# Sixteen products without use in front of the second unit's key norm, in both halves of a hybrid decoder block

## The chip, the cores and the metric

The kernel runs on one core of one Trainium2 chip. The metric is the device time of one execution in microseconds; of several executions the median counts. The engines are named as in the profile: PE (TensorE), PEld (its weight loads), DVE (VectorE), ACT (ScalarE), POOL (GpSimd) and SP (SyncE, which issues most transfers).

## What is computed

One decoder layer on a sequence of 1024 tokens with 1024 channels, all in fp32. The conditioning vector c gives shift, scale and gate of two sub-layers. The first is a token mixer of two parallel branches:

```python
h = rms_norm(x, norm1_gain) * (1 + scale1) + shift1
proj = h @ w_in
cols = proj[..., :q_lo]; cols = cols + (token_shift(cols) - cols) * tshift_mu
y_a = rwkv7_time_mix(cols, ...)        # 8 heads of 64, delta-rule state
y_b = sliding_window_sink_attention(...)   # 8 query heads, window 128
merged = gate_a * (y_a @ w_branch_a) + gate_b * (y_b @ w_branch_b)
x = x + gate1 * (merged @ w_out)
```

The second is a SwiGLU feed-forward block. In the RWKV branch each head's key direction is divided by its length; this is the key norm:

```python
kk = heads(k * k_k)
kk = kk / jnp.maximum(jnp.sqrt(jnp.sum(kk * kk, axis=-1, keepdims=True)), 1e-12)
```

## The kernel before, in words

**Halves and units.** The mixer goes through two halves of 512 tokens (the loop over h), and in each through four units (p = 0 to 3), a unit being two RWKV heads on 128 partitions. The branch projections to 1024 channels, the output projection and the feed-forward block follow.

**Products.** An fp32 product is made of three: both operands are split into a high and a low part, and `mm3` (L138 to L144) issues low weight by high activation, high by low, and high by high, each a matmul of 128x512. `proj_block` (L473) makes one block of 128 columns of `w_in` from eight such triples, 24 products, in a PSUM tile `pg` of a pool of two. Each unit starts with three such blocks: key, receptance, value, in this order. `shifted` (L483) then mixes each with its neighbour token: a copy on ACT (`tm`, L489), two small copies on POOL, and one operation on DVE (`rvk`, L491).

**The unit.** `rwkv_unit` (L494) starts with two low-rank products, `pz` (L499) and `paa` (L505). ACT takes `pz` through a tanh into `sz` (L501) and `paa` into `ath` (L507). POOL and DVE make the cumulated decay `cum` of `sz` (L511), and ACT its exponentials, `wpad` (L515) and `winv` (L517). Then ACT squares the scaled keys (`sq`, L522), and PE sums the squares of each head: `ns` (L524), a product of fp32 operands, which the trace shows as two passes. ACT copies its two rows to `nrow` (L526), and they go through memory to the later stages. Further products of the unit are `bs` (L561, from `ath` on DVE), `pa` and `pk`. `pz`, `paa`, `ns`, `bs`, `pa` and `pk` share a PSUM pool `pm` of two buffers, so each waits until the tile two before it has been read.

**Work beside it.** `ada_rest` (L872 to L886) makes the rest of the conditioning, eight times a call, one call for each unit: SP loads a tile `adaw` (L883, one buffer), ACT scales it (L884), POOL adds it (L885). ACT goes through its instructions in order, so all that stands behind L884 waits for that load. Attention is dealt in between the units (`mixer_step`); the keys of an attention block are rounded by ACT to `kdup` (L802), DVE makes the low part `klo` (L803), and PE makes the scores `sc` (L827).

**What sets the order.** The code is written unit by unit; a tile scheduler, which has a model and priorities of its own, deals the instructions to each engine's order when the kernel is built. An instruction that is added or tied to another changes what is dealt behind it.

Of the kernel before, what the change touches and what calls it, by code (L numbers as in the profile page):

```python
# [10 lines left out]
F32 = mybir.dt.float32  # L11
# [8 lines left out]
P = 128  # L20
D = 1024
S = 1024
HALF = 512
NH = 2
KT = D // P
RW = 512
NP = 4
NPOOL = 3
NC = HALF // 64
DFF = 2816  # L30
NJ = DFF // P
# [35 lines left out]
def block_kernel(ctx: ExitStack, tc: tile.TileContext, a: dict, out: bass.AP):  # L67
    nc = tc.nc
# [15 lines left out]
    def vcol(name, i=0, n=1):  # L84
        st, r0, cnt = ROWS[name]
        return vT[st][:, r0 + i:r0 + i + n]
# [53 lines left out]
    def mm3(ps, lh, ll, rh, rl, first, last, more=False):  # L140

        nc.tensor.matmul(ps, lhsT=ll, rhs=rh, start=first, stop=False, skip_group_check=more)  # L142
        nc.tensor.matmul(ps, lhsT=lh, rhs=rl, start=False, stop=False, skip_group_check=more)  # L143
        nc.tensor.matmul(ps, lhsT=lh, rhs=rh, start=False, stop=last, skip_group_check=more)  # L144

    gates_d = dr.tile([NH, 16, P, HALF], F32, name="gates_d")
    ya_d = dr.tile([NH, NP, P, HALF], F32, name="ya_d")
    yb_d = dr.tile([NH, NP, P, HALF], F32, name="yb_d")
    a_scr = dr.tile([NH, NP, 2, NC, 2, 32, 32], F32, name="a_scr")
    t_scr = dr.tile([NH, NP, 2, NC, 2, 32, 32], F32, name="t_scr")  # L150
    n_scr = dr.tile([NH, NP, 2, HALF], F32, name="n_scr")
# [25 lines left out]
    with ExitStack() as mx:  # L177
# [5 lines left out]
        pm = mx.enter_context(tc.tile_pool(name="pm", bufs=2, space=PSUM))  # L183
# [84 lines left out]
        with tc.tile_pool(name="su", bufs=1, side="right") as su:  # L268
# [24 lines left out]
            def ada_columns(g, wts):  # L293

                pcol = pc.tile([P, 4], F32, tag="pc", name="pcol")
                for sec in range(2):
                    acc = su.tile([P, 256], F32, tag="adacc", name="adacc", bufs=3)
                    if sec == 0 and g < NPOOL:
                        nc.gpsimd.memset(acc, 0.0)
# [5 lines left out]
                    else:  # L305
                        nc.vector.tensor_scalar(out=acc, in0=wts[sec][:, 0, :],
                                                scalar1=vcol("c", 0), scalar2=None, op0=ALU.mult)
                    for k in range(1, 0 if sec == 0 and g < NPOOL else KT):
                        nc.vector.scalar_tensor_tensor(out=acc, in0=wts[sec][:, k, :],
# [40 lines left out]
            blk1 = wc.tile([P, P], F32, name="blk1")  # L350
# [122 lines left out]
        def proj_block(hT, j):  # L473

            wh, wl = w_block(j)
            del w_ahead[j]
            pool, tag = first_psum.pop(j, (pg, "pg"))
            ps = pool.tile([P, HALF], F32, tag=tag, name="pg")
            for k in range(KT):
                mm3(ps, wh[:, k, :], wl[:, k, :], hT[k][0], hT[k][1], k == 0, k == KT - 1)  # L480
            return ps

        def shifted(hT, j, dst):  # L483

# [6 lines left out]
                nc.vector.scalar_tensor_tensor(out=dst, in0=ps, scalar=ommu[:, j:j + 1],  # L491
                                               in1=tm[:, 0:HALF], op0=ALU.mult, op1=ALU.add)

        def rwkv_unit(h, p, rvk, xwa, sgx):  # L494
            r_, v_, k_ = (rvk[:, i, :] for i in range(3))

            ch = slice(p * P, (p + 1) * P)
# [22 lines left out]

            sq = wk.tile([P, HALF], F32, tag="early", name="sq", bufs=5)
            nc.scalar.activation(out=sq, in_=k_, func=AF.Square, scale=vcol("k_k", p))  # L522
            ns = pm.tile([2, HALF], F32, tag="pm", name="ns")
            nc.tensor.matmul(ns, lhsT=blk1[:, 0:P:64], rhs=sq, start=True, stop=True)  # L524
            nrow = wk.tile([2, HALF], F32, tag="early", name="nrow", bufs=5)
            nc.scalar.copy(out=nrow, in_=ns)  # L526
            nc.sync.dma_start(out=n_scr[h, p], in_=nrow)
# [40 lines left out]
            for b in range(2):  # L568
                pas = [pm.tile([P, 4, P], F32, tag="pm", name="pa") for _ in range(2)]
                for c4 in range(4):  # L570
                    c = 4 * b + c4
                    for q in range(2):
                        rows = slice(64 * q, 64 * q + 64)
                        nc.tensor.matmul(pas[q][:, c4, :], lhsT=kb[rows, c, q:q + 2, :],
                                         rhs=ar[rows, c, :, :], start=True, stop=True)
# [30 lines left out]
            for sl in range(2):  # L606
# [5 lines left out]
                for jj in range(16):  # L612
# [3 lines left out]
                    m, n = j // 4 + 1, 31 - j  # L616
# [24 lines left out]
            for c in range(NC):  # L641
                for q in range(2):
                    u0 = 64 * (1 - q)
                    nc.tensor.matmul(pv1[u0 + 32:u0 + 64, c, :],
                                     lhsT=asb[q][u0:u0 + 32, c, 32:64], rhs=tn[u0:u0 + 32, c, :],
                                     start=True, stop=True)
# [3 lines left out]
            for c in range(NC):  # L650
                for q in range(2):
                    u0 = 64 * (1 - q)
                    nc.tensor.matmul(pt1[u0:u0 + 32, c, :], lhsT=v1[u0 + 32:u0 + 64, c, :],
                                     rhs=tt[u0 + 32:u0 + 64, c, 32:64], start=True, stop=True)
# [4 lines left out]
            for c in range(NC):  # L659
                g = G[p]  # L660
                zp = pc.tile([P, 64], F32, tag="pc", name="zp")
                for q in range(2):
# [3 lines left out]
                                     start=True, stop=False)  # L666
                for q in range(2):
# [3 lines left out]
                                     start=False, stop=True)  # L671
# [5 lines left out]
                up = pc.tile([P, 64], F32, tag="pc", name="up")  # L677
                for q in range(2):
# [3 lines left out]
                                     start=True, stop=True)  # L682
# [3 lines left out]
                for q in range(2):  # L686
                    rows = slice(64 * q, 64 * q + 64)
                    nc.tensor.matmul(gp[rows, :], lhsT=kbt[q][:, c, :], rhs=vu[q][:, c, :],
                                     start=True, stop=True)
# [4 lines left out]
                for q in range(2):  # L694
                    rows = slice(64 * q, 64 * q + 64)
                    nc.tensor.matmul(yps[rows, c, :], lhsT=ar[rows, c, 1, :], rhs=g[rows, :],
                                     start=True, stop=False)
                for q in range(2):
                    rows = slice(64 * q, 64 * q + 64)
                    nc.tensor.matmul(yps[rows, c, :], lhsT=asb[q][:, c, 64:128], rhs=vu[q][:, c, :],  # L700
                                     start=False, stop=True)
# [16 lines left out]
            for q in range(2):  # L718
                rows = slice(64 * q, 64 * q + 64)
                pt = py.tile([P, NC, 64], F32, tag="py", name="pyt")  # L720
                for c in range(NC):
# [4 lines left out]
                    elif lo_ < 0:  # L726
                        nc.tensor.matmul(pt[64:128, c, :], lhsT=ycf[rows, 0:64],
                                         rhs=ident[rows, rows], start=True, stop=True)
# [166 lines left out]
        for h in range(NH):  # L895
            if h == 0:
                hT = hT0
            else:
                hT = []
# [9 lines left out]
            xwa = wk.tile([P, HALF], F32, tag="xwa", name="xwa", bufs=1)  # L909
            shifted(hT, 12, xwa)  # L910
            nc.scalar.activation(out=xwa[0:64, :], in_=xwa[0:64, :], func=AF.Tanh)
            sgx = wk.tile([P, HALF], F32, tag="sgx", name="sgx", bufs=1)
# [4 lines left out]
            for p in range(NP):  # L917
                mixer_step(h, p, hT)
                rvk = wk.tile([P, 3, HALF], F32, tag="rvk", name="rvk", bufs=2)
                for i, j in ((2, 4 + p), (0, p), (1, 8 + p)):  # L920
                    shifted(hT, j, rvk[:, i, :])
                rwkv_unit(h, p, rvk, xwa, sgx)
                if h == 0:
                    if p == 0:
                        rotary_tables()
                    prepare_x(p)
                ada_rest(4 * h + p)
# [17 lines left out]
            for j in range(16):  # L945
                ps = proj_block(hT, 20 + j)
# [523 lines left out]
```

## Time and profile before

| | |
|---|---|
| median of three runs | 1655.84 us (1649.59 to 1656.13) |
| profiled execution | 1638.24 us |
| its span | 1636.5 us |
| mean granted clock of PE in it | 0.989 |
| PE busy | 1553.0 us (95%), 8835 matmuls |
| DVE busy | 1192.2 us (73%) |
| ACT busy | 709.1 us (43%) |
| POOL busy | 156.1 us (10%) |
| chain of work that ended last | PE 73%, DVE 11%, DMA 6%, ACT 4% |

Busy shares are means over the span. The granted clock of PE stands as a share of its full speed: 1.00 is 2.4 GHz, and 0.50 is 1.2 GHz. The page counts a matmul of 128x512 with the time from its start to the end of its flow; the spacing of two starts is shorter, since matmuls overlap.

### The profile page before, as it was taken

The page shows a single profiled execution, that of the slowest core. Times are in us where ns is not written, and L with a number is a line of the kernel's source. Part 1 is how long each engine was busy: PE and PEld are TensorE (multiplying, and loading weights), DVE is VectorE, ACT ScalarE, POOL GpSimd, SP SyncE. Part 2 cuts the span into 40 slices and gives each one's busy share as a digit, 9 for nine tenths or more (in the row PEclk, how much of TensorE's full clock was granted, in tenths as well). Part 3 has the DMA queues.
Part 4 walks back from the last instruction along what each step waited for, and adds up shares of the span by engine and source line. Part 5 has one row for each costly group of instructions (what it writes and reads, how often), then busy time and mean ns, then how long its engine had stood idle before and what let it go on. Part 6 is the DMA issues. An engine that isn't in the chain of part 4 may idle for free.

```text
span 1636.5 us, 24815 instructions
## 1 busy us (share of the span) xinstructions
PE 1553.0 (95%) x8835; PEld 1195.9 (73%) x8835; DVE 1192.2 (73%) x2844; ACT 709.1 (43%) x1346; POOL 156.1 (10%) x220
## 2 busy tenths in 40 slices
PE   3978999999998999999999998999999999999998
PEld 2756776666665678667778886788888888888887
DVE  6689777877557868877368877976666677897465
ACT  6454343555744333446411566423333333444442
POOL 6223121212343000000000000000000000000000
PEclk9999999999999999999999999999999999999999
DMA  9345444544544323324583146253333232974441
GB/s 320 101 120 146 123 139 121 155 128 145 152 139 112 85 69 95 99 86 146 167 282 119 59 157 223 87 171 104 103 97 104 97 102 94 313 242 131 149 142 52
DMA packets 225502, 223.97 MB, mean 137 GB/s; under 512 B 38466, under 2 KB 162508, under 8 KB 225380
## 3 DMA queue, kind: packets, MB, share of 16 engines
q1 hardware_dynamic: 225380, 222.41, 44.4%
q8 instruction: 69, 1.13, 0.3%
q14 instruction: 53, 0.43, 0.1%
HBM read 171.73 MB, written 50.63 MB: 136 GB/s over the span
## 4 chain that ended last, share of the span: by engine, by line
PE 73%; DVE 11%; DMA 6%; ACT 4%; issue 2%; POOL 2%; SPq 1%; ACTq 0%; DVEq 0%; POOLq 0%
PE pgf L142 10%; PE pgf L143 10%; PE pgf L144 10%; PE pgo L144 6%; PE pgo L143 6%; PE pgo L142 6%; DMA adaw<-in_ada_w_dram 4%; PE pg L142 4%; PE pg L143 4%; PE pg L144 4%; PE pgq L142 1%; PE pgq L144 1%; PE pgq L143 1%; DVE rt L623 1%; DVE tmpi L619 1%
## 5 line engine op out<-in xcount | busy, mean ns | idle before, releaser
L142 PE MATMUL pg<-hhi,wlo 128*128 128x512 f32 x480 | 201.0, 421 | 2.0 <-DVE xwa L491 0.9
L143 PE MATMUL pg<-hlo,whi 128*128 128x512 f32 x480 | 198.8, 414 | 0.0
L144 PE MATMUL pg<-hhi,whi 128*128 128x512 f32 x480 | 198.2, 413 | 0.0
L144 PE MATMUL pgo<-wpart 128*128 128x512 f32 x420 | 163.9, 390 | 0.0
L143 PE MATMUL pgo<-wpart 128*128 128x512 f32 x420 | 163.8, 390 | 0.0
L142 PE MATMUL pgo<-wpart 128*128 128x512 f32 x420 | 163.3, 390 | 0.0
L133 ACT CAST whi<-wraw 128x1024 fp32r<-128x1024 f32 (+1 forms) x88 | 85.0, 967 | 98.2 <-PE pgf L144 45.0
L134 DVE TENSOR_TENSOR wlo<-wraw,whi 128x1024 fp32r<-128x1024 f32 (+1 forms) x88 | 100.9, 1146 | 26.0 <-ACT whi L133 18.0
L885 POOL TENSOR_TENSOR aacc<-aacc,adaw 128x512 f32<-128x512 f32 x64 | 90.6, 1416 | 257.6 <-ACT adaw L884 246.8
L142 PEld LDWEIGHTS pg<-hhi,wlo 128*128 128x128 f32 x480 | 92.5, 193 | 28.4 <-issue 6.7
L1066 DVE TENSOR_TENSOR u<-pgf,u 128x512 f32<-128x512 f32 x88 | 60.5, 689 | 68.0 <-PE pgf L144 67.1
L144 PEld LDWEIGHTS pg<-hhi,whi 128*128 128x128 f32 x480 | 92.8, 193 | 22.2 <-issue 3.3
L143 PEld LDWEIGHTS pg<-hlo,whi 128*128 128x128 f32 x480 | 92.9, 193 | 19.2 <-issue 1.3
L1061 ACT CAST wpart<-s 128x512 fp32r<-128x512 f32 x88 | 54.7, 622 | 111.0 <-PE pgf L144 99.8
L1061 ACT CAST wpart<-fo 128x512 fp32r<-128x512 f32 x77 | 48.0, 624 | 113.9 <-PE pgo L144 107.9
L1062 DVE TENSOR_TENSOR wpart<-fo,wpart 128x512 fp32r<-128x512 f32 x77 | 52.8, 687 | 52.4 <-ACT wpart L1061 52.3
L143 PEld LDWEIGHTS pgo<-wpart 128*128 128x128 f32 x420 | 78.8, 188 | 16.3 <-issue 0.2
L144 PEld LDWEIGHTS pgo<-wpart 128*128 128x128 f32 x420 | 78.9, 188 | 16.2
L142 PEld LDWEIGHTS pgo<-wpart 128*128 128x128 f32 x420 | 78.8, 188 | 16.2
L1061 ACT CAST wpart<-wraw 128x512 fp32r<-128x512 f32 x66 | 40.6, 622 | 101.3 <-PE pgf L144 98.6
L619 DVE SCALAR_TENSOR_TENSOR tmpi<-ai,inv,rt 128x60 f32<-128x60 f32 (+24 forms) x248 | 74.3, 300 | 10.6 <-DMA ai<-a_scr 6.9
L884 ACT ACTIVATE adaw<-adaw,vT 128x512 f32<-128x512 f32 x64 | 46.2, 722 | 73.2 <-DMA adaw<-in_ada_w_dram 67.7
(507 smaller groups left out, 3807.3 us busy)
## 6 DMA issues: line engine op xcount, KB each, us to landing
wraw<-in_w_in_dram SPq DMA_DIRECT2D x72, 512.0 KB
wraw<-in_ffn_w_dram SPq DMA_DIRECT2D x56, 512.0 KB
f_d<-fs SPq DMA_DIRECT2D x77, 256.0 KB
fo<-f_d SPq DMA_DIRECT2D x77, 256.0 KB
adaw<-in_ada_w_dram SPq DMA_DIRECT2D x64, 256.0 KB
w2t<-in_ffn_w_dram SPq DMA_DIRECT2D x44, 256.0 KB
adaw<-in_ada_w_dram SPq DMA_DIRECT2D x8, 1024.0 KB
gates_d<-gt SPq DMA_DIRECT2D x32, 256.0 KB
```

The costliest lines, as they stand in the source:

```text
L133: nc.scalar.copy(out=hi, in_=raw)
L134: nc.vector.tensor_tensor(out=lo, in0=raw, in1=hi.bitcast(F32), op=ALU.subtract)
L142: nc.tensor.matmul(ps, lhsT=ll, rhs=rh, start=first, stop=False, skip_group_check=more)
L143: nc.tensor.matmul(ps, lhsT=lh, rhs=rl, start=False, stop=False, skip_group_check=more)
L144: nc.tensor.matmul(ps, lhsT=lh, rhs=rh, start=False, stop=last, skip_group_check=more)
L619: nc.vector.scalar_tensor_tensor(out=tv, in0=ai[:, jj, j + 1:32].unsqueeze(1).broadcast_to([P, m, n]), scalar=inv2[:, j:j + 1], in1=rt[:, ...
L623: nc.vector.tensor_tensor(out=rt[:, 0:m, j + 1:32], in0=rt[:, 0:m, j + 1:32], in1=tv, op=ALU.add)
L884: nc.scalar.activation(out=wt, in_=wt, func=AF.Copy, scale=vcol("c", k))
L885: nc.gpsimd.tensor_tensor(out=acc, in0=acc, in1=wt, op=ALU.add)
L1061: nc.scalar.copy(out=hi, in_=src)
L1062: nc.vector.tensor_tensor(out=lo, in0=src, in1=hi.bitcast(F32), op=ALU.subtract)
L1066: nc.vector.tensor_tensor(out=out, in0=x, in1=y, op=op)
```

## The change

With `WARM` = 16, `proj_block` keeps the last product of the latest block (`proj_end`; for a unit this is its value block). In unit 1 of each half `keep_warm` takes a tile `pwarm` of `pm` and issues 16 products of 128x512 into it, all with the same weights (the first 128 columns of the first high part of the activations) and each with the high part of another block as its moving operand. Nothing reads them. Each is tied behind the one before it, the first behind `proj_end`, and `ns` behind the last of them, by a dependency that sets only the order.

```diff
+WARM = 16
...
             for k in range(KT):
-                mm3(ps, wh[:, k, :], wl[:, k, :], hT[k][0], hT[k][1], k == 0, k == KT - 1)
+                end = mm3(ps, wh[:, k, :], wl[:, k, :], hT[k][0], hT[k][1], k == 0, k == KT - 1)
+            proj_end[0] = end
             return ps
+
+        proj_end = [None]
+
+        def keep_warm(hT, n):
+
+            ps = pm.tile([P, HALF], F32, tag="pm", name="pwarm")
+            behind = proj_end[0]
+            for i in range(n):
+                mm = nc.tensor.matmul(ps, lhsT=hT[0][0][:, 0:P], rhs=hT[i % KT][0], start=True,
+                                      stop=True)
+                tc.add_manual_dep(mm.ins, behind.ins.name,
+                                  mybir.DependencyInfo(mybir.DependencyClass.NoSync,
+                                                       mybir.DependencyReason.DATA),
+                                  reason="right behind the projections")
+                behind = mm
+            return behind
...
             nc.scalar.activation(out=sq, in_=k_, func=AF.Square, scale=vcol("k_k", p))
+            warm = keep_warm(hT, WARM) if p == 1 else None
             ns = pm.tile([2, HALF], F32, tag="pm", name="ns")
-            nc.tensor.matmul(ns, lhsT=blk1[:, 0:P:64], rhs=sq, start=True, stop=True)
+            mm = nc.tensor.matmul(ns, lhsT=blk1[:, 0:P:64], rhs=sq, start=True, stop=True)
+            if warm is not None:
+                tc.add_manual_dep(mm.ins, warm.ins.name,
+                                  mybir.DependencyInfo(mybir.DependencyClass.NoSync,
+                                                       mybir.DependencyReason.DATA),
+                                  reason="behind the products that keep the clock up")
```

PE gets 32 instructions more. Its order is the one of before up to the first of the new products and again for its last 3329 instructions; between them the mixer's instructions are dealt anew on every engine. In the changed file the lines stand 1 lower from L30 on, 18 lower around `pz` and 24 lower behind `ns`.

PE in the first half, from `pz` of the second unit to its `ns`, before (27 products `pg` in nine triples, of which the first two and the last stand here):

```order
L499 MATMUL pz<-xwa,diu 128x512
L505 MATMUL paa<-xwa,diu 128x512
L142 MATMUL pg<-hhi,wlo 128x512
L143 MATMUL pg<-hlo,whi 128x512
L144 MATMUL pg<-hhi,whi 128x512
L142 MATMUL pg<-hhi,wlo 128x512
L143 MATMUL pg<-hlo,whi 128x512
L144 MATMUL pg<-hhi,whi 128x512
...
L142 MATMUL pg<-hhi,wlo 128x512
L143 MATMUL pg<-hlo,whi 128x512
L144 MATMUL pg<-hhi,whi 128x512
L524 MATMUL ns<-sq,blk_463 2x512
```

and after:

```order
L145 MATMUL pg<-hhi,whi 128x512
L492 MATMUL pwarm<-hhi 128x512 x16
L143 MATMUL pg<-hhi,wlo 128x512
L144 MATMUL pg<-hlo,whi 128x512
L145 MATMUL pg<-hhi,whi 128x512
L143 MATMUL pg<-hhi,wlo 128x512
L144 MATMUL pg<-hlo,whi 128x512
L145 MATMUL pg<-hhi,whi 128x512
L143 MATMUL pg<-hhi,wlo 128x512
L144 MATMUL pg<-hlo,whi 128x512
L543 MATMUL ns<-sq,blk_463 2x512
```

Ahead of these rows `pz`, `paa` and one triple stand as before, of which the first row here is the last product. So 11 products `pg` stand between `paa` and `ns` where 27 stood, and 16 stand behind `ns` that stood in front of it.

PE in the second half, same place, after:

```order
L517 MATMUL pz<-xwa,diu 128x512
L523 MATMUL paa<-xwa,diu 128x512
L143 MATMUL pg<-hhi,wlo 128x512
L144 MATMUL pg<-hlo,whi 128x512
L145 MATMUL pg<-hhi,whi 128x512
L492 MATMUL pwarm<-hhi 128x512 x16
L543 MATMUL ns<-sq,blk_463 2x512
```

Before, 17 products `pg` stood between `paa` and `ns` there and no others; 14 of them have moved behind `ns`. In both halves the first `pwarm` waits for a signal of ACT, the end of `sz`, which reads `pz` out of the buffer that `pwarm` takes.

ACT around the keys of the first attention block, before:

```order
L792 CAST qs_3863<-pq 64x512
L949 ACTIVATE gt<-pg,hbg 128x512
L605 COPY rt<-idpat 128x256
L884 ACTIVATE adaw_3419<-adaw_3419,vT_67 128x512
L802 CAST kdup_529<-pkT 64x128 x2
L802 CAST kdup_530<-pkT 64x128 x2
```

and after:

```order
L816 CAST qs_3877<-pq 64x512
L816 CAST qs_3880<-pq 64x512
L826 CAST kdup_529<-pkT 64x128 x2
L134 CAST whi<-wraw 128x1024
L826 CAST kdup_530<-pkT 64x128 x2
L672 COPY v_2399<-pv_2398 32x256 x2
L908 ACTIVATE adaw_3436<-adaw_3436,vT_67 128x512
```

The scaled copy of a load of `adaw` that stood right in front of `kdup` is behind it now. Elsewhere on ACT the opposite happened: in front of the third unit's `tm` and `sz` of the first half, where one copy of `adaw` stood, there are two. The orders of ACT and SP up to `sq` of the second unit in the first half are the ones of before.

## Rows read from the trace of the kernel before

**Rows 1.** The page, its span and its first part.

```profile
span 1636.5 us, 24815 instructions
...
PE 1553.0 (95%) x8835; PEld 1195.9 (73%) x8835; DVE 1192.2 (73%) x2844; ACT 709.1 (43%) x1346; POOL 156.1 (10%) x220
```

**Rows 2.** Waits of PE: engine, line, waited for; us in total, times, longest.

```profile
PE ns L524 <- ACT sq L522: 16.2, 6, 6.1
...
PE sc L827 <- DVE klo L803: 4.3, 1, 4.3
```

**Rows 3.** PE timeline, first half: start us, us, what, [idle before, releaser].

```profile
112.98 0.40 PE L144 MATMUL pg<-hhi,whi 128*128 128x512 f32 x1
119.51 1.86 PE L524 MATMUL ns<-sq,blk 128*2 128x512 f32 x2 [6.13 <-ACT sq L522]
121.31 0.80 PE L142 MATMUL pg<-hhi,wlo 128*128 128x512 f32 x1
...
124.86 0.40 PE L144 MATMUL pg<-hhi,whi 128*128 128x512 f32 x1
```

**Rows 4.** PE timeline, second half, around the second unit's key norm.

```profile
503.72 0.40 PE L144 MATMUL pg<-hhi,whi 128*128 128x512 f32 x1
503.96 0.39 PE L142 MATMUL pg<-hhi,wlo 128*128 128x512 f32 x1
504.19 0.40 PE L143 MATMUL pg<-hlo,whi 128*128 128x512 f32 x1
509.56 1.86 PE L524 MATMUL ns<-sq,blk 128*2 128x512 f32 x2 [4.97 <-ACT sq L522]
511.35 0.80 PE L144 MATMUL pg<-hhi,whi 128*128 128x512 f32 x1
...
514.02 0.40 PE L144 MATMUL pg<-hhi,whi 128*128 128x512 f32 x1
```

**Rows 5.** PE timeline, third unit of the first half.

```profile
150.30 1.02 PE L524 MATMUL ns<-sq,blk 128*2 128x512 f32 x2 [1.84 <-ACT sq L522]
...
161.57 1.34 PE L561 MATMUL bs<-ath,blk 128*128 128x512 f32 x2 [3.04 <-DVE ath L558]
...
163.56 0.63 PE L144 MATMUL pg<-hhi,whi 128*128 128x512 f32 x1
163.99 0.63 PE L142 MATMUL pg<-hhi,wlo 128*128 128x512 f32 x1
```

**Rows 6.** ACT timeline, first half, second unit.

```profile
110.11 0.69 ACT L501 ACTIVATE sz<-pz,hw 128x512 f32<-128x512 f32 x1
...
117.61 0.72 ACT L884 ACTIVATE adaw<-adaw,vT 128x512 f32<-128x512 f32 x1 [4.17 <-DMA adaw<-in_ada_w_dram]
...
118.75 0.70 ACT L522 ACTIVATE sq<-rvk,vT 128x512 f32<-128x512 f32 x1
```

**Rows 7.** ACT timeline, second half, second unit.

```profile
500.93 0.69 ACT L501 ACTIVATE sz<-pz,hw 128x512 f32<-128x512 f32 x1
...
506.53 0.72 ACT L884 ACTIVATE adaw<-adaw,vT 128x512 f32<-128x512 f32 x1 [4.34 <-POOL wpad L514]
```

**Rows 8.** Windows: us, PE, PEld, DVE, ACT, POOL busy (instructions), clock, DMA share, GB/s.

```profile
119.50:124.70 5.20, 5.19 (x10) 2.81 (x11) 5.02 (x10) 2.76 (x4) 1.77 (x3) 0.50 0.17 51
...
150.30:158.30 8.00, 8.00 (x32) 5.65 (x32) 6.88 (x25) 3.32 (x7) 1.20 (x3) 1.00 0.55 150
162.40:165.70 3.30, 3.30 (x9) 2.32 (x8) 3.30 (x14) 0.00 (x0) 0.00 (x0) 0.50 0.18 66
...
509.60:513.80 4.20, 4.20 (x8) 2.01 (x9) 4.09 (x12) 1.20 (x2) 1.06 (x1) 0.50 0.21 63
...
113.00:165.00 52.00, 40.33 (x185) 27.39 (x184) 47.28 (x137) 24.59 (x40) 14.01 (x19) 0.91 0.50 132
560.00:760.00 200.00, 198.40 (x1783) 143.63 (x1783) 154.30 (x592) 82.94 (x195) 3.04 (x9) 1.00 0.30 87
```

**Rows 9.** ACT timeline in front of the first attention block's keys.

```profile
285.03 0.72 ACT L884 ACTIVATE adaw<-adaw,vT 128x512 f32<-128x512 f32 x1 [4.82 <-DMA adaw<-in_ada_w_dram]
```

**Rows 10.** PE timeline, that block's scores.

```profile
288.14 0.30 PE L827 MATMUL sc<-klo,qs 128*128 128x128 f32 x1 [4.29 <-DVE klo L803]
```

More of the change, by code (lines that the diff above doesn't have):

```diff
@@ L143, in mm3 @@
         nc.tensor.matmul(ps, lhsT=lh, rhs=rl, start=False, stop=False, skip_group_check=more)
-        nc.tensor.matmul(ps, lhsT=lh, rhs=rh, start=False, stop=last, skip_group_check=more)
+        return nc.tensor.matmul(ps, lhsT=lh, rhs=rh, start=False, stop=last, skip_group_check=more)
     gates_d = dr.tile([NH, 16, P, HALF], F32, name="gates_d")
@@ L492, in shifted, with rwkv_unit @@
                                                in1=tm[:, 0:HALF], op0=ALU.mult, op1=ALU.add)
-        def rwkv_unit(h, p, rvk, xwa, sgx):
+        def rwkv_unit(h, p, rvk, xwa, sgx, hT):
             r_, v_, k_ = (rvk[:, i, :] for i in range(3))
@@ L921, in block_kernel @@
                     shifted(hT, j, rvk[:, i, :])
-                rwkv_unit(h, p, rvk, xwa, sgx)
+                rwkv_unit(h, p, rvk, xwa, sgx, hT)
                 if h == 0:
```

## The prediction

> **What bounds the kernel now.** I read the page first. PE is busy for 95% of the span and no other engine for more than 73% [rows 1], so almost all that PE does, it does on the path. The waits of PE came second. They show where PE stands still: the largest sum is its wait for `sq` in front of the key norm `ns`, 16.2 us in six times, the longest 6.1 [rows 2]. The timelines place two of the six in the second units: 6.13 us in the first half and 4.97 in the second [rows 3, 4]. Together that is 11.1 us of idle time in front of the two places that the change touches.
>
> Third came the clock. Behind the two waits the granted clock is 0.50, the lower level (1.2 GHz), for some 5.2 and 4.2 us [rows 8], where it was at full speed before the wait; `ns` then takes 1.86 us, while the third unit's `ns`, which came after an idle time of 1.84 us at a clock of 1.00, takes 1.02 [rows 5, 8]. Behind an idle time of 3.04 us in front of `bs` the clock is 0.50 too [rows 5, 8].
>
> Last, what PE waits for. `sq` is in order behind a scaled copy of `adaw` on ACT, which in the first half waited 4.17 us for its load and starts at 117.61; `sq` follows at 118.75 and ends at 119.45, when `ns` begins [rows 3, 6]. In the second half the copy waited 4.34 us for POOL [rows 7]. Neither wait is for PE. So products put in front of `ns` can't bring `ns` forward; all they can change is the clock behind it, and what PE has left to do there. Around the first place the second bound is near: DVE is busy for 47.28 of 52 us, 91% [rows 8].
>
> **Prices.** At full speed products of 128x512 start 0.2333 us apart (503.72 to 504.19 in two steps) [rows 4], at the lower level 0.43 us apart (163.56 to 163.99) [rows 5]. The new products are of that shape, so 16 take 3.73 to 6.88 us. The Trainium skill, "TensorE: Matmul & The Clock Gate", section "Wait — 56ns, not 53.3ns?", gives 215.7 ns for this spacing on a fast clock; by it the 16 would take 3.45 us, but the row is 8% longer, and the row decides.
>
> **The change, first half.** The first new product waits for the end of `sz`, 110.11 + 0.69 = 110.80 [rows 6]. In the order of after, three products `pg` stand ahead of it. In the trace the last of the 27 starts at 112.98, so the fourth started some 23 x 0.2333 earlier, at 107.6 [rows 3, 4]: PE now stands still from 107.6 to 110.8, about 3.2 us, before the new products begin. That is next to the 3.04 us after which the clock was at 0.50 for 3.3 us [rows 5, 8], so I let the first 8 products go at 0.43 and the rest at 0.2333: 3.4 + 1.9 = 5.3 us, to 116.1. Eight useful products follow, 1.9 us, to 118.0, and 1.5 us are left until `sq` ends. That is next to the 1.84 us after which the clock stayed up, so `ns` and what follows go at full speed. The gain is then 1.86 − 1.02 = 0.84 on `ns`, and on the eight products behind it (121.31 to 124.86 took 3.55, at full speed 8 x 0.2333 = 1.87) 1.68: together **−2.5**. If the clock falls after all, it is 0. Sixteen useful products that were hidden in the idle time now stand behind `ns`: 16 x 0.2333 = **+3.7**. Net +1.2, bounds 0 and +3.7. The third unit has waits of its own for ACT and DVE, 1.84 + 3.04 = 4.9 us [rows 5]; I take their chains not to be lengthened by PE's delay, and then a delay of 1.2 fits into them. I take **0**.
>
> **Second half.** `sz` ends at 500.93 + 0.69 = 501.62 [rows 7], and the fourth of the 17 products started 13 x 0.2333 before 504.19, at 501.16 [rows 4]. So the new ones start with hardly a wait, at full speed, and end at 501.62 + 3.73 = 505.4. `ns` waits until 509.56 still, 4.2 us, which lies nearer to the 4.97 and the 3.04, after both of which the clock fell [rows 4, 5, 8], than to the 1.84. I credit 0; the most would be 0.84 for `ns` and, for six products from 511.35 to 514.02, 2.67 − 1.40 = 1.27, together −2.1. Fourteen useful products go behind `ns`: 14 x 0.2333 = **+3.3**. PE is busy for 198.4 of 200 us from 560 to 760 [rows 8]: nothing later takes that up. Bounds +1.2 and +3.3.
>
> **The order dealt anew.** Two places stand out. At the first attention block `kdup` stood behind a copy of `adaw` that waited 4.82 us for its load [rows 9], and PE waited 4.29 us in front of the scores [rows 10]. That copy is now behind `kdup`. The wait should go, and with it a stretch at the lower clock that I price like those above, by 1.3 to 1.7 us, 1.5: **−5.8**, bounds 0 (another late tile takes its place) and −6. Against it, the third unit's `tm` and `sz` in the first half have one more copy of `adaw` in front of them on ACT. Waits on such a load were 4.17 and 4.82 [rows 6, 9]; that unit's `ns` waits for what follows from them, so I take somewhat less than these, **+4.0**; bounds 0 (the load has landed by then) and +4.8 with a slow stretch of 1.7 on top, +6.5.
>
> **Sum**: 0 + 3.3 − 5.8 + 4.0 = +1.5 us. The profiled execution took 1638.24 us (span 1636.5 and 1.7 around it), so 1639.7. The median of the runs, 1655.84, lies 17.6 us (1.1%) above it; put on that, +1.5 gives **1657 us**.
>
> **Rivals.**
>
> 1. *The clock stays up in both halves*, and what is displaced fits into waits that were there. The 4.2 us left in the second half speak against it, the 1.84 us row for it. All credits, no cost: −2.5 − 2.1 = −4.6, about 1651; where the `kdup` wait goes as well with nothing in its place, −10.4, 1645. The Trainium skill has the rule for it (the page named above, "Why this matters for your kernels"): leave no long idle gaps between bursts of matmuls, else throughput drops in mid-kernel. The trace agrees that it drops, 1.86 against 1.02 us for `ns`. What the rule doesn't say is who pays for the work that the filler displaces.
>
> 2. *Slower: the third unit's chain in the first half grows at its start.* I took it that PE's delay does not lengthen that chain. But the displaced products make the projection blocks of the next unit, from which its `tm` and `rvk` start. If DVE, 91% busy there [rows 8], does not hold these up anyway, the chain starts 3.7 us later; the second copy of `adaw` on ACT then adds 4.8 and a slow stretch of 1.7 behind a longer wait, the second half its 3.3, and the load that is late in front of `kdup` now is late in front of some other tile, so that nothing comes back: 3.7 + 6.5 + 3.3 = +13.5, **1669**. It decides if the blocks' end, and not DVE's backlog, sets when `rvk` of the third unit starts. For it: waits of more than 4 us in front of three such copies [rows 6, 7, 9]. Against it: DVE's share, and that the third unit's `ns` lost only 1.84 us with a copy of `adaw` ahead of it on ACT.
>
> 3. *The `kdup` wait goes and nothing comes in its place*: 3.3 − 5.8 = −2.5, 1653.
>
> 4. *The change doesn't do what it says*: the clock falls behind both `ns` as before, since ACT's wait is far longer than 16 products. Then 3.7 + 3.3 − 5.8 + 4.0 = +5.2, 1661.
>
> **How the numbers follow.** Chances: forecast 0.45, rival 1 0.16, rival 2 0.17, rival 3 0.12, rival 4 0.10. A change of 0.5%, 8.3 us, is about what a measurement of this kernel can tell from none. Faster by that: half of rival 1 (with the `kdup` wait gone), 0.08, and 0.05 for other waits of the newly dealt mixer that go without my having priced them: 0.13. Slower: rival 2, 0.17, and 0.03 for such waits that come: 0.20. Within it: 0.67. The range goes from 1645 (rival 1) to 1669 (rival 2), and by 3 us further at each end, half of the 6.5 us between the runs shown: 1642 to 1672.
>
> **What would show it.** Clock and length of both `ns`: right is 1.00 and about 1.0 us in the first half, 0.50 and 1.9 in the second. Idle time in front of the first new product: 3.2 us, then 0.4. Idle time in front of `ns`: 1.5 and 4.2 where 6.13 and 4.97 stood. The wait at the scores gone; a new wait of ACT on `adaw` near 140 us that reaches PE. I am wrong if the sum of PE's idle time in the mixer changes by more than some 10 us at a place that I did not name, or if the displaced products cost nothing.

## Result: slower by 1.2%, and the profile after

The change takes 1670.65 us (median of four runs, 1665.89 to 1673.53) where the kernel before took 1655.25 us in the same comparison: a ratio of 1.0124, 95% interval 1.0086 to 1.0162. The two medians lie 15.4 us (0.9%) apart, which is within that interval; 1.24% would be some 20 us. I had forecast 1657. The median lies within the range given, at its far end, in the place of the slower rival.

The two places that the change touches came out much as worked out. PE timeline of the kernel after, first half:

```profile
110.97 5.54 PE L492 MATMUL pwarm<-hhi 128*128 128x512 f32 x16 [3.11 <-ACT sz L519]
116.35 0.39 PE L143 MATMUL pg<-hhi,wlo 128*128 128x512 f32 x1
...
119.12 1.02 PE L543 MATMUL ns<-sq,blk 128*2 128x512 f32 x2 [0.75 <-ACT sq L540]
120.07 0.50 PE L145 MATMUL pg<-hhi,whi 128*128 128x512 f32 x1
```

and second half:

```profile
515.85 3.94 PE L492 MATMUL pwarm<-hhi 128*128 128x512 f32 x16 [0.34 <-ACT sz L519]
524.43 1.87 PE L543 MATMUL ns<-sq,blk 128*2 128x512 f32 x2 [4.64 <-ACT sq L540]
526.23 0.80 PE L143 MATMUL pg<-hhi,wlo 128*128 128x512 f32 x1
```

The 16 products wait 3.11 us for `sz`, start slow, fill the wait, and the first half's key norm runs at full speed in 1.02 us behind 0.75 us of idle time, where [rows 3] had 6.13 and 1.86. In the second half they run fast, 4.64 us are left, and the norm takes 1.87 as in [rows 4]. So these waits came out as forecast, and the loss is behind them or elsewhere. The waits of PE, the answer to [rows 2]:

```profile
PE ns L543 <- ACT sq L540: 13.6, 6, 5.4
...
PE pgf L144 <- DVE y_0l L165: 5.0, 1, 5.0
PE up L705 <- DVE zs L697: 4.5, 4, 2.7
PE pwarm L492 <- ACT sz L519: 3.5, 2, 3.1
...
PE sc L851 <- DVE klo L827: 0.5, 2, 0.3
```

The wait at the scores is gone (4.3 to 0.5). The key norms still wait 13.6 us, although 6.13 became 0.75: the longest is now 5.41, in the fifth unit (the first of the second half). New waits stand at `up`, and at `y_0l`, which is not in the mixer at all but in the stage of the branch projections.

By stages: from 103.5 us, just ahead of the second unit, to the first product `pgf` of the branch stage; from there to the first `pgo`; and a like length behind it. Columns as in [rows 8]. The windows of before:

```profile
103.50:808.60 705.10, 667.21 (x4907) 474.90 (x4906) 516.66 (x1672) 339.79 (x697) 112.38 (x138) 0.98 0.43 123
808.60:904.80 96.20, 94.41 (x421) 77.48 (x422) 71.86 (x118) 16.89 (x29) 0.00 (x0) 0.98 0.62 197
904.80:1631.00 726.20, 718.89 (x3175) 589.59 (x3174) 527.64 (x876) 299.93 (x525) 0.00 (x0) 1.00 0.42 135
```

and of after:

```profile
103.50:833.60 730.10, 685.83 (x4939) 485.02 (x4937) 520.14 (x1672) 337.81 (x696) 115.63 (x138) 0.97 0.41 118
833.60:938.30 104.70, 96.04 (x420) 77.78 (x421) 72.86 (x119) 17.43 (x30) 0.00 (x0) 0.95 0.60 189
938.30:1664.50 726.20, 718.84 (x3170) 589.72 (x3169) 527.86 (x876) 300.41 (x525) 0.00 (x0) 1.00 0.41 135
```

The mixer takes 25.0 us more: PE is busy 18.6 us longer (9.5 of it in the 32 products, 5.54 and 3.94) and idle 6.4 longer. The branch stage takes 8.5 more; the rest is equal. That makes 34 us between these two executions, more than the 15 to 20 of the comparison, since the profiled execution of before was a quick one (experiment 1).

Two theories. **Theory 1**: the products cost next to nothing; the order that the scheduler dealt anew costs. **Theory 2**: the products cost, by their own time and the useful work that they displace. The second half of theory 2 needs care: the displaced work, 16 and 14 useful products that stand behind the norms now, is itself a part of the new order.

### The profile page after: what moved, and what is told of

Read it like the earlier page. It is cut to its first block, busy times and chain, and to the rows that moved or that the text cites. A ratio compares the mean times of both kernels' runs of the same rounds, so it can differ in the third digit from the quotient of the medians.

```text
span 1671.0 us, 24859 instructions
## 1 busy us (share of the span) xinstructions
PE 1574.5 (94%) x8867; PEld 1207.6 (72%) x8867; DVE 1197.6 (72%) x2844; ACT 707.9 (42%) x1346; POOL 159.4 (10%) x220
## 4 chain that ended last, share of the span: by engine, by line
PE 72%; DVE 12%; DMA 8%; ACT 4%; issue 2%; POOL 2%; SPq 1%; ACTq 0%; DVEq 0%; POOLq 0%
PE pgf L143 9%; PE pgf L144 9%; PE pgf L145 9%; PE pgo L145 6%; PE pgo L144 6%; PE pgo L143 6%; PE pg L145 4%; PE pg L144 4%; PE pg L143 4%; DMA adaw<-in_ada_w_dram 3%; PE pa L598 2%; PE pgq L144 2%; PE pgq L143 2%; PE pgq L145 2%; DVE wlo L135 1%
## 5 line engine op out<-in xcount | busy, mean ns | idle before, releaser
L135 DVE TENSOR_TENSOR wlo<-wraw,whi 128x1024 fp32r<-128x1024 f32 (+1 forms) x88 | 101.1, 1149 | 28.0 <-ACT whi L134 27.1
```

The source lines that it names most:

```text
L135: nc.vector.tensor_tensor(out=lo, in0=raw, in1=hi.bitcast(F32), op=ALU.subtract)
```

## Experiments

All ratios are to the kernel before, in runs of the same session.

**1. The order held fast.** To tell order from products, an order was written into the kernel: a table holds for each engine the places, in program order, of its instructions, and each is tied behind the one before by a dependency that sets only the order.

```diff
+def pin_order(tc, fillers):
+    rows = [i for i in tc.nc.cur_bb.bb.instructions if i.name not in fillers]
...
+    for order in issue_orders():
+        for one, two in zip(order, order[1:]):
+            tc.add_manual_dep(rows[two], rows[one].name, step, reason="issue order")
...
         block_kernel(tc, args, o)
+        pin_order(tc, set())
```

> The kernel before, with its own order of instructions held fast on every engine. Both theories: no difference, a ratio of 1.000 within 0.004. It gives a second profiled execution of the order of before: the first mixer's stage ended 25.0 us earlier there than in the changed kernel (the first product pgf at 808.6 against 833.6); I expect 805 to 820 here, and a granted clock of 0.985 to 0.99.

Measured: 1.0010 (0.9981 to 1.0039), as expected; the first `pgf` came at 818.5, within the 805 to 820. It taught more than that. The same order in another execution, the same stretch around the start of the first half's fourth unit, once in the profile of before and once in this one:

```profile
217.00:240.00 23.00, 22.59 (x215) 15.79 (x214) 19.88 (x55) 14.11 (x26) 6.45 (x6) 1.00 0.36 116
```

```profile
217.00:240.00 23.00, 23.00 (x118) 13.33 (x117) 13.53 (x39) 8.98 (x17) 3.37 (x5) 0.51 0.29 94
```

In 23 us PE does 215 matmuls at a clock of 1.00, or 118 at 0.51. No wait of half a microsecond stands in front of that stretch in either execution. The kernels with 24 products (experiment 2) and of experiment 6, which keep this order nearly as it is, have such a stretch of 24 us there too; the one with 16 has none. The time of one order varies from run to run (1634 to 1658 us over the runs of before), so two traces must not be subtracted stage by stage without a second pair.

**2. The products in the order of before.** Order held fast, 16 or 24 products directly in front of both key norms, behind the useful ones.

```diff
+            if rows[two].name in first_filler:
+                tc.add_manual_dep(first_filler[rows[two].name], rows[one].name, step,
+                                  reason="fillers behind it")
```

> The order of before on every engine, held fast, with the 16 products directly in front of both key norms, behind all useful products that stood there. Theory 1: no loss; 0 to 4 us faster than before (ratio 0.997 to 1.000), the key norms at 119 and 509 us take 1.0 us at full clock in the first half (about 2.4 us idle left in front) and perhaps in the second (about 1.2 us left). Theory 2: the products by themselves cost, 4 to 10 us slower, ratio 1.003 to 1.006.

> As the kernel with 16, with 24 products, 5.6 us, which nearly fills the 6.13 us and overfills the 4.97 us in front of the two key norms. Theory 1: full clock behind both, 2 to 4.6 us faster than before, less up to 0.7 us by which the second half's products outlast the wait; ratio 0.997 to 1.000. Theory 2: slower than with 16, ratio 1.004 to 1.008.

Measured: 1.0016 (0.9985 to 1.0048) and 1.0018 (0.9985 to 1.0050). No loss that shows, so the products' own time costs nothing in this order; the other half of theory 2 is not tested here, since no useful product is displaced. And no gain either, though both second units' key norms ran at full speed. Where the gain went, the PE timeline of the kernel with 16 shows in the second half:

```profile
506.18 3.80 PE L523 MATMUL pwarm<-hhi 128*128 128x512 f32 x16
510.21 1.02 PE L575 MATMUL ns<-sq,blk 128*2 128x512 f32 x2 [0.23 <-ACT sq L572]
...
521.25 2.04 PE L620 MATMUL bs<-ath,blk 128*128 128x512 f32 x2 [2.83 <-DVE ath L617]
```

PE is through its useful products earlier, but `bs` waits for DVE, which the products don't hasten: it starts 11.04 us behind `ns`, as before (11.10), the idle time in front of it grows to 2.83 us (0.87 in before), and there the clock falls. From 522 to 535 us:

```profile
522.00:535.00 13.00, 13.00 (x66) 9.74 (x65) 9.61 (x23) 3.91 (x6) 1.64 (x3) 0.52 0.30 85
```

From this `pz` to the next unit's it took 39.05 us (501.06 to 540.11), where the two executions without products took 35.56 and 35.84. In the first half the same distance was 35.24 against 37.18 and 36.62. Gained 1.4 to 1.9, lost 3.2 to 3.5. The kernel with 24 products has 35.52 and 39.89, the same picture; there `bs` waits 2.58 us, and the clock falls some 5 us later.

**3. The order of after without the products.** They are left out, and only their order kept.

> The order of the changed kernel on every engine, held fast, without the 32 products of no use. Theory 1 (the order dealt anew is what costs, by sparse stretches of PE at the lower clock): slower than before by 10 to 20 us, ratio 1.006 to 1.012, with the low-clock stretches near 132 to 146 us and 231 to 241 us as in the changed kernel. Theory 2 (the products cost, by their own time and the useful ones they displace): within 4 us of before, ratio 0.997 to 1.003.

> The order of the changed kernel on every engine without the products, with the first half's key norm in its own place: in the earlier kernel of this kind it stood eight useful products too early, directly behind the three that follow paa. Leaving them behind the norm can cost at most their own 1.9 us and a longer low stretch behind the longer wait (13.7 us at 0.50 were seen there, against 6.8 in the order of before: 3.4 us). If the order alone carries the loss, the ratio is 1.009 to 1.014; if the misplaced norm carried much of the 1.014, it is 1.003 to 1.008, and the products and their wait for sz carry the rest of the change's 1.0124.

Measured: 1.0140 (1.0092 to 1.0188), and 1.0101 (1.0065 to 1.0136) with the norm in its place, which is the one that counts: the loss is there without a single product. The stretches at the lower clock that theory 1 named did not come: the exact kernel has one of 3 us near 135 us, and neither has one at 231 to 241 us. Stages of the exact one:

```profile
103.50:827.70 724.20, 674.59 (x4906) 477.45 (x4904) 520.54 (x1670) 337.73 (x697) 116.58 (x138) 0.97 0.40 119
827.70:930.70 103.00, 96.49 (x421) 77.93 (x422) 73.19 (x119) 17.36 (x30) 0.00 (x0) 0.95 0.60 193
```

The order held in experiment 1, at the same mixer clock of 0.97, took 715.0 with PE busy for 676.8. So the mixer's order of after costs 9.2 us here, and it is idle time: 49.6 us where 38.2 stood. That is no accident of one execution: the four kernels with this order and no products (experiments 3 to 5) have 48.9 to 50.9 us of idle time in the mixer, the two executions of the order of before 37.9 and 38.2.

Where in the mixer? Between `pz` of the second unit and `pz` of the third PE has the same products in both orders. This took 42.37 us in the exact kernel (105.71 to 148.08), against the 37.18 and 36.62 of experiment 2, and in the second half 37.60 (504.50 to 542.10), against 35.56 and 35.84. So 7.0 to 7.8 us of the loss stand at the two places of the change, where useful products were moved behind the norms. This experiment does not tell that displaced work from the rest of the new order; the last pair of experiment 7 does.

**4. The branch stage.** For all that stands behind the mixer in the program, the table of before; for the mixer, that of after, without and with the products. (In both, and in experiment 5, the first half's norm stands eight useful products early, as in the first kernel of experiment 3.)

> The order of the changed kernel for the mixer, without the products, and the order of before for what comes behind it in the program (the branch projections, the output projection, the loads for them). In two executions of the order of after the stage from the first product pgf to the first pgo took 101.1 and 104.7 us, in four of the order of before 95.0 to 97.6. If the order of that stage's loads and low parts causes it, the stage takes 95 to 98 us here, and the whole is 4 to 8 us less than with the order of after throughout (ratio 1.008 to 1.011 to before, where that had 1.014). If the late end of the mixer causes it, it stays at 101 to 105 and the ratio at 1.014.

> As the kernel with the mixer's order of the change and the branch stage's order of before, with the 32 products in the places that they have in the change. Theory 1 (products as such cost nothing and gain nothing that can be measured, in either order): within 0.004 of 1.0091. Theory 2: 0.004 or more slower, 1.013. If keeping the clock up at the two key norms were worth the 4.6 us credited to it at most, 1.006.

Measured: 1.0091 (1.0062 to 1.0120) and 1.0093 (1.0060 to 1.0125). The branch stage took 95.2 and 95.6 us, so behind this mixer it is its order that made it 101 to 105, and PE's idle time in it fell from 8.7 to 1. And products or none is the same in this order too. How the stage is held up shows in the kernel after. Its SP issues, its DVE and its PE:

```profile
874.75 1.46 SPq L1202 DMA_DIRECT2D wo<-in_w_out_dram  x3
876.26 1.85 SPq L172 DMA_DIRECT2D yst<-ya_d  x4
```

```profile
897.47 0.68 DVE L1090 TENSOR_TENSOR mg<-mg,gt 128x512 f32<-128x512 f32 x1
898.07 0.68 DVE L165 TENSOR_TENSOR y_0l<-yst,y_0h 128x512 fp32r<-128x512 f32 x1
```

```profile
898.80 0.79 PE L144 MATMUL pgf<-y_0l,whi 128*128 128x512 f32 x1 [5.02 <-DVE y_0l L165]
```

SP issues the loads `yst` 42.7 us into the stage (876.26 − 833.6), behind the output projection's weights; before, they were issued from 33.7 us on (842.30 − 808.6). DVE then makes `y_0l` behind a row of operations on `mg`, `gt` and `wo`, and PE waits 5.02 us; the granted clock is 0.50 from 893 to 903 us.

**5. The fifth unit.** Its norm waited longest. ACT and PE of the kernel after:

```profile
482.16 0.72 ACT L908 ACTIVATE adaw<-adaw,vT 128x512 f32<-128x512 f32 x1 [4.25 <-DMA adaw<-in_ada_w_dram]
482.79 0.67 ACT L507 ACTIVATE tm<-pg,vT 128x512 f32<-128x512 f32 x1
...
484.30 0.69 ACT L519 ACTIVATE sz<-pz,hw 128x512 f32<-128x512 f32 x1
```

```profile
489.38 1.87 PE L543 MATMUL ns<-sq,blk 128*2 128x512 f32 x2 [5.41 <-ACT sq L540]
```

A copy of `adaw` stands in front of `tm` and `sz` and waits 4.25 us. Moved behind `ath` in ACT's table, in the first kernel of experiment 4:

```
-adaw2_7064
 tm_5205
 whi_5796
 sz_5212
 ath_5217
+adaw2_7064
```

> The kernel with the mixer's order of the change (no products) and the branch stage's order of before, with one more copy moved on ACT: of the two copies of adaw that stand in front of tm and sz of the fifth unit (first unit of the second half), the second goes behind ath, where it stood before. In the order of after it waited 4.2 us for its load there, and that unit's key norm had 4.9 to 5.4 us idle in front of it, against 1.1 to 1.5 in the order of before. If this copy is the cause, that idle time falls to under 2 us, and the whole is 2 to 6 us less than without the move: ratio 1.005 to 1.008 where that had 1.0091. If the idle time only goes to the next wait, the ratio stays within 0.002 of 1.009.

Measured: 1.0089 (1.0054 to 1.0125), no gain, and the norm still waits 3.95 us (4.88 in the first kernel of experiment 4). DVE's `cum` now waits for POOL. POOL and DVE:

```profile
484.33 1.28 POOL L910 TENSOR_TENSOR aacc<-aacc,adaw 128x512 f32<-128x512 f32 x1 [3.58 <-ACT adaw L909]
...
485.95 0.62 POOL L527 TENSOR_SCALAR sz<-sz 128x512 f32<-128x512 f32 x1
```

```profile
486.60 1.22 DVE L536 TENSOR_TENSOR_SCAN cum<-cmask,sz 128x512 f32<-128x512 f32 x1 [3.65 <-POOL sz L527]
```

The edit moved the copy on ACT alone. On POOL the addition of the same `adaw` kept its place in front of POOL's own step on `sz`, so `cum`, and with it `sq` and the norm, still waits for the late load. So this run does not show that the load is harmless; no run moved both.

**6. Waits taken away in the order of before.** No products; the copies of `adaw` in front of `sq` [rows 6] and of `kdup` [rows 9] go behind them.

```
 wpad_1461
-adaw2_1328
 winv_1464
 sq_1468
+adaw2_1328
...
-adaw2_3419
 kdup0_529 x2
 kdup1_530 x2
+adaw2_3419
```

> The order of before on every engine, no products, with two copies on ACT moved: the copy of adaw that stood in front of winv and sq in the second unit of the first half goes behind sq, and the one in front of kdup in the first attention block goes behind the four kdup casts. So the waits are taken away and not filled. Expected if a wait that is taken away is kept: ns of that unit starts some 4.5 us earlier, its idle time 6.1 falls to 1 or 2 and the clock stays up, the 4.3 us in front of the scores go to under 0.5: 6 to 12 us faster, ratio 0.993 to 0.997. If the idle time only goes to the next wait of PE for DVE or ACT (DVE is 91% busy around the first place): ratio 0.998 to 1.001.

Measured: 1.0019 (0.9989 to 1.0049): nothing gained. The PE timeline:

```profile
115.06 1.02 PE L549 MATMUL ns<-sq,blk 128*2 128x512 f32 x2 [1.18 <-ACT sq L547]
...
123.32 0.50 PE L167 MATMUL pg<-hhi,wlo 128*128 128x512 f32 x1 [2.15 <-DVE wlo L159]
...
128.15 1.13 PE L586 MATMUL bs<-ath,blk 128*128 128x512 f32 x2 [2.93 <-DVE ath L583]
```

The norm starts at 115.06, 4.5 us earlier, as expected, and the wait at the scores is gone too; but PE waits 2.15 and 2.93 us for DVE, where the kernel before has no wait at either place, and in this execution the clock falls behind these. Some 9 us of waits were taken away, and PE's idle time in the mixer is 35.3 us where 37.9 and 38.2 stood. The clock:

```profile
131.00:149.00 18.00, 18.00 (x81) 13.64 (x81) 10.80 (x36) 4.85 (x8) 3.08 (x3) 0.50 0.38 108
```

**7. Other deals.** The change with fewer products, or in one half, dealt by the scheduler.

```diff
-WARM = 16
+WARM = 1
```

```diff
-            warm = keep_warm(hT, WARM) if p == 1 else None
+            warm = keep_warm(hT, WARM) if p == 1 and h == 1 else None
```

> The changed kernel with 1 product in place of 16 in each half, dealt freely by the scheduler. Its own work is 0.23 us a half, so what it costs or gains is the deal. Theory 1 (each deal anew is a throw of its own, and the tuned order of before is a good one): away from before by more than 4 us, most likely slower, ratio 1.003 to 1.015. Theory 2 (the products and what they displace cost): within 0.003 of 1.000. No product at all with the same tie of the key norm behind the projections leaves the order of before as it is on every engine.

> The 16 products in the second half alone, dealt freely; the order of the first half stands as before. Theory 1: the places of the first half (a longer wait in front of pq and the chain's products near 286 us, the pxt waits near 157 us) are as before, the wait of 5.4 us in front of the fifth unit's key norm is as before too (1.1 to 1.5), so only the second unit of the second half and the branch stage can differ: ratio 1.000 to 1.006. Theory 2: half of the whole loss, 1.006.

> The 16 products in the first half alone, dealt freely. The second half alone gave 1.0053, both 1.0124. If the two halves' deals add up, 1.007 here. The branch stage tells by itself: 101 us or more from the first pgf to the first pgo with a wait of 4 to 5 us for y_0l where its loads are dealt as in the change, 95 to 98 where as in before.

Measured: one product 1.0005 (0.9973 to 1.0037), the second half alone 1.0053 (1.0015 to 1.0091), the first alone 1.0111 (1.0067 to 1.0155). All deal the order anew. Theory 1 as I had put it, that a new deal most likely costs, was too strong: the deal for one product costs nothing that shows. The second half alone fits both theories, and the first alone is above the 1.007 that adding the halves would give. In the first-half kernel the branch stage took 102.3 us with 4.9 us of wait for `y_0l`, as in the change; in the second-half kernel 96.2. What the deals differ in at the two places is the displaced work: with one product both norms keep nearly all their useful products in front of them; in the second half alone 14 stand behind the norm, in the first alone 16.

Last, that deal with the branch stage's order of before and without the product:

> The mixer's order of the kernel with one product, which lost nothing in the mixer but had the longer branch stage (100.9 us, 4.5 us of wait for y_0l), with the branch stage's order of before, and no product. If the orders of the two stages are independent, the branch stage takes 95 to 98 us and the whole is 3 to 6 us faster than before: ratio 0.996 to 0.999.

> The mixer's order of the kernel with one product, without the product, key norms in their own places (in the earlier kernel of this kind the first half's norm stood 29 useful products, 6.8 us, too early), and the branch stage's order of before. If the misplaced norm made the 1.0093: idle time in front of the second unit's key norm of 4 to 6 us, where 11.57 stood, and a ratio of 0.996 to 1.001. If the mixer's order of that deal costs without the product too: 1.005 or more.

Measured: 1.0093 (1.0060 to 1.0126) with the norms too early, by a wrong place in the table, and 1.0010 (0.9985 to 1.0035) with them in their places. The hoped-for gain is missing: the branch stage took 101.1 us still, now with 3.8 us of wait for `wlo`, so the order of before does not make this stage short behind every mixer.

The wrong place is a measurement of its own, and the cleanest one of displaced work. The two kernels have one and the same order on ACT, DVE, POOL and SP; on PE they differ in the places of the second units' norms alone. PE's timelines show 23 useful products moved behind the norm in the first half (not the 29 of the expectations) and 14 in the second. With them moved:

```profile
118.56 1.87 PE L549 MATMUL ns<-sq,blk 128*2 128x512 f32 x2 [11.57 <-ACT sq L547]
520.81 1.87 PE L549 MATMUL ns<-sq,blk 128*2 128x512 f32 x2 [9.45 <-ACT sq L547]
```

and in their places:

```profile
118.75 1.87 PE L549 MATMUL ns<-sq,blk 128*2 128x512 f32 x2 [6.31 <-ACT sq L547]
510.48 1.87 PE L549 MATMUL ns<-sq,blk 128*2 128x512 f32 x2 [6.34 <-ACT sq L547]
```

From `pz` of the second unit to that of the third it took 48.38 us (104.97 to 153.35) against 37.13 (105.06 to 142.19), and in the second half 40.19 (509.34 to 549.53) against 36.59 (498.85 to 535.44): 14.9 us more, and the two executions differ by 13.4 (1665.12 and 1651.76). The 37 products themselves are 8.6 us at 0.2333 us each. The rest is the clock: its mean over the two stretches is 0.75 and 0.83, against 0.91 and 0.91. So useful work moved behind a norm that waits costs more than its own time, and the whole is longer by nearly as much.

No kernel beat the one before.

## Why the prediction was wrong

**Right: the two places.** The wait for `sz` (3.2 said, 3.11 measured; 0.4 and 0.34), the first products slow and the end at 116.1 (116.35), idle time in front of the norms (1.5 and 4.2; 0.75 and 4.64), their clocks, full and half. The useful products that were displaced weigh what I said: in the order of after without products the norms wait 9.19 and 8.32 us, against 5.5 and 5.2 in the order of before (experiment 1), 3.7 and 3.2 more, for 3.7 and 3.3 predicted. The second half's term, +3.3, came too: from `pz` to `pz` the kernel after takes 38.39 us there (513.48 to 551.87), 2.55 to 2.83 more than the order of before. (The rows cited for the spacing give 0.235 us, not 0.2333, which is what longer runs of products show; nothing hangs on it.)

**Wrong: the first half, put at 0.** The prediction had +1.2 there and let the third unit's waits take it up, since it took "their chains not to be lengthened by PE's delay". They are lengthened. ACT and DVE of the kernel after, at the start of the third unit:

```profile
145.71 0.69 ACT L507 ACTIVATE tm<-pg,vT 128x512 f32<-128x512 f32 x1 [2.10 <-PE pg L145]
```

```profile
146.44 0.75 DVE L509 SCALAR_TENSOR_TENSOR rvk<-pg,ommu,tm 128x512 f32<-128x512 f32 x1 [3.84 <-ACT tm L507]
```

DVE waits 3.84 us for `tm`, and `tm` 2.10 us for PE's block; in the kernel before, this `tm` waited 0.54 us and `rvk` not at all. The third unit's `pz` comes 45.37 us behind the second's (105.84 to 151.21), 8.2 to 8.8 more than in the order of before. A stretch at the lower clock (0.52 from 131.0 to 144.7) is a part of that; the second kernel of experiment 4, with nearly the same mixer and the products, has no such stretch and takes 40.49 us (105.71 to 146.20), 3.3 to 3.9 more. The third unit's own waits did shrink, by 3.6 us (`ns` 1.84 to 1.00, `bs` 3.04 to 0.24), but a wait of 2.34 us at `pxt` came; the delay was not taken up.

**Wrong: the order dealt anew, put at −5.8 + 4.0.** The order by itself costs 1.01% (0.65 to 1.36), 16.6 us. By single executions, 7.0 to 7.8 of these are the displaced work at the two places (experiment 3) and 6.8 to 7.7 the branch stage (103.0 against 96.2 and 95.3); all else, waits that went and waits that came, leaves little, and was not measured by itself. I priced two places that I had found by reading rows of the order and took the sum of two for the sum of all. Of the two, `kdup` was right: the wait at the scores went. In the third unit the second copy of `adaw` did wait for its load. ACT and PE of the kernel after:

```profile
153.20 0.73 ACT L908 ACTIVATE adaw<-adaw,vT 128x512 f32<-128x512 f32 x1 [5.24 <-DMA adaw<-in_ada_w_dram]
```

```profile
157.13 0.66 PE L248 MATMUL pxt<-ident,xs 128*128 128x128 f32 x4 [2.34 <-ACT xst L251]
```

It reaches PE in another place and by less than the +4.0: `ns` waits 1.00 us, less than in [rows 5], and `pxt` 2.34 us for `xst`, which stands behind `adaw`, `tm` and `sz` on ACT. The other waits that came were not on my list: `ns` of the fifth unit (1.45 to 5.41), `up` (2.73 at 627 us), `pq` (1.78 at 287 us), and `y_0l` in the branch stage.

**Wrong: "nothing later takes that up".** It was right of the second half's displaced work, but the same reading put all that stands behind the mixer at nothing. I looked at PE, whose last 3329 instructions are the same, and did not look at SP and DVE, which serve that stretch and are dealt anew in it. The branch stage's 8.5 us are half of a per cent; putting its order back took the loss from 1.0140 to 1.0091, though these intervals overlap.

**The credits.** Up to 2.5 and 2.1 us for the clock were of the right size for the norm and its neighbours. What failed in the second half is that they are kept: where the order was held and both norms ran at full speed, 1.4 to 1.9 us were gained in the first half, and 3.2 to 3.5 lost behind `bs` in the second.

**The rivals.** Rival 2's number, 1669, came out, in part for its reasons. Its condition held: the blocks' end, and not DVE's backlog, set when the third unit's `rvk` starts, and its terms for the displaced work, 3.7 and 3.3, are in the trace. Of its 6.5 for the second copy of `adaw` 2.34 us reached PE, its lost `kdup` gain did not come true (that wait went), and the branch stage is not in it. So the sum was luck. Whether the late load in front of the fifth unit's `tm` and `sz` costs anything stays open (experiment 5). Rival 1's clock was made to happen in experiment 2, with nothing displaced, and no gain showed. The Trainium skill, "TensorE: Matmul & The Clock Gate", section "Why this matters for your kernels", asks for no long idle gaps between bursts; the traces agree that the clock falls behind such gaps (the products behind 3.11 us of idle time took 5.54 us, those behind 0.34 took 3.94), and in the second half of experiment 2 they add that with the next wait set by another engine, the fall is put off and not saved.

**Open.** What the new waits away from the two places cost was not settled; the one edit that aimed at one of them left its load in the chain. How much of the 16.6 us is displaced work is read from single executions here; that such work costs is shown by the last pair of experiment 7, in a neighbouring order. Runs of the order of before spread by 1.5%, so differences under some 5 us stay open.

## What to carry to other kernels

Where a scheduler deals the order, an inserted instruction is two changes: its own work, and a new order for everything behind it. Hold the order fast and measure each alone; here the products were worth 0 (within 0.5%) and the order 1%. Look first at what useful work the new order moved behind a wait: 37 products moved behind two norms cost 14.9 us where their own time is 8.6. Compare the orders of all engines to the end of the program, loads included, and where an engine's wait is filled or taken away, look at who sets its next one before counting the gain.

## What was not expected of the hardware

The clock of one and the same order differs between executions in stretches without a notable wait: 217 to 240 us ran at 1.00 in one and at 0.51 in another, 215 matmuls against 118. Nor does the length of an idle time alone tell what follows. In the second kernel of experiment 4 two waits of nearly the same length stand 9 us apart:

```profile
110.78 5.51 PE L520 MATMUL pwarm<-hhi 128*128 128x512 f32 x16 [3.05 <-ACT sz L548]
119.43 1.02 PE L572 MATMUL ns<-sq,blk 128*2 128x512 f32 x2 [3.14 <-ACT sq L569]
```

Behind 3.05 us the products start at the lower clock; behind 3.14 us `ns` runs at full speed. My reading of "nearest row" for the clock was right twice by luck.
